# A two-layer encoder whose down projection works with seven products: sums of activations made in other rows, summed weight chunks taken ahead of chained ones

## The chip, the cores and the metric

The kernel runs on one core of one Trainium2 chip. A core has a matrix engine (TensorE, PE in the profile, with its weight loads shown as PEld), a vector engine (VectorE, DVE), an activation engine (ScalarE, ACT), GpSimd (POOL) and a sync engine (SyncE, SP) that here only issues DMAs. Each engine works through its own queue of instructions. Where an instruction needs the result of another engine, it waits at the head of its queue, and what stands behind it waits too. Matrix products are accumulated in PSUM. Operands lie in SBUF, and the weights come from HBM by DMA.

The metric is device microseconds of one execution. Lower is better.

## The reference

Two layers work on x of 256 positions by 2048 features. The even layer mixes by pooling and attention and the odd one by an mLSTM. Neither is touched. Each layer ends in a gated MLP (5632 hidden features), and the change lies there:

```
def conv_ffn(x, w_up, conv_w, conv_b, w_down):
    u = x @ w_up                                  # 2048 -> 2 x 5632
    up = jnp.pad(u, ((0, 0), (1, 1), (0, 0)))
    u = c[0] * up[:, :-2] + c[1] * up[:, 1:-1] + c[2] * up[:, 2:] + conv_b
    gate, val = jnp.split(u, 2, axis=-1)
    return (jax.nn.silu(gate) * val) @ w_down     # 5632 -> 2048

x = x + conv_ffn(rms_norm(x, norm_ffn[layer]), w_up[layer], conv_w[layer], conv_b[layer], w_down[layer])
```

Everything is float32 in the reference.

## The kernel before, in words

**Precision.** A float32 operand is split into a high part (a cast to the matrix engine's format) and a low part (the rest), and a product is made of three matmuls: high by high, high by low, low by high. For a weight chunk of 128 by 1024 the high part is a cast on ScalarE (line 127) and the low part a subtraction on VectorE (line 128). Both write one tile named `hl`, of which there are four. So a chunk can be split only after TensorE is done with the one four before it. The class `Stream` holds the list of chunks in the order in which TensorE takes them. It loads them up to five ahead into six tiles `w` (line 107, SyncE's queue) and splits them up to two ahead.

**The MLP.** The 44 tiles of hidden features are worked through in groups of 4, 8, 8, 8, 8, 8 (`FCH`), called c = 0 to 5. For one tile, `up` makes a group of 64 matmuls from four weight chunks (gate and value). Its result then goes through these steps: `gather` copies one half from PSUM (ACT line 426) and adds the other (DVE line 427), VectorE multiplies by the norm (line 983), ScalarE makes six scaled copies (lines 988 to 990, twice each), VectorE adds them with a shift of one position (lines 991 and 992), then come silu (ACT 996), the product with the value (DVE 997), and the high and low parts (ACT 998, DVE 999).

**The down projection.** For the hidden tiles of c = 0 to 4 a pair of hidden tiles, two halves of 128 positions and two blocks of 512 output columns form a two-by-two block product, which is made with seven block products instead of eight. This needs sums of activations and sums of weights. `combine` (called "mix" in the plan) makes the four sums of activations of one pair: `sf` on VectorE (lines 1005 to 1007), high parts on ScalarE (line 1011) and low parts on VectorE (line 1012), into `s3` (three sums) and `s1` (the fourth).

The products of one group are made in units. A unit A makes the four products 4, 6, 5, 3 of its pairs, and a unit B the three products 0, 1, 2. For the column half h = 1, a unit A takes two kinds of weight chunks for each pair:

- a summed chunk (`Sum`): one block is loaded by SyncE (line 112) and another is added to it on the way by a DMA of GpSimd (line 113), in a tile `sum`, of which there are three. It serves products 4 and 6.
- a chained chunk (`Chain`): it is loaded like any weight. VectorE then adds half of the summed chunk to its first half (line 123, kept on VectorE's queue behind the low part of the chunk before by `behind`) and the first half to the second (line 124), before it is split. It serves products 5 and 3.

For h = 0 both are read ready made from a buffer in HBM (`Made`), which DMAs fill earlier (`premix`, line 472).

**The plan.** `_ffn_plan` writes the order out: a row is one `up`, then at most one unit of the group before (in the first groups sometimes a plain block of the down projection too), then the mixes of that row. Where both column halves go by seven products (c = 2, 3, 4 in layer 0 and c = 1 to 4 in layer 1, `BOTH`), a unit has two pairs. Group c is then multiplied in the eight rows of group c + 1: A for h = 1 with pairs 0, 1 and then 2, 3 (rows 0 and 1), B likewise (rows 2 and 3), then A and B for h = 0 (rows 4 to 7). After the last unit of an A or a B, `drain` adds the accumulated products from PSUM to x or to `acc` (DVE line 1068). Elsewhere a unit has one pair. There are seven groups with units of two pairs and h = 1, so seven rows 0 and seven rows 1 of this kind.

**What sets the order.** TensorE's queue is the order of the program. The other engines' queues are put in order by the framework's scheduler, from its own picture of when an operand is ready, so an instruction's place in the source does not fix its place on VectorE or ScalarE.

Of the kernel before, what the change touches and what calls it, by code (L numbers as in the profile page):

```python
# [9 lines left out]
F32 = mybir.dt.float32  # L10
# [6 lines left out]
P = 128  # L17
# [21 lines left out]
ATT_PARTS = [[4 + h for h in range(8)], [0, 1, 2, 3], [4 + h for h in range(8, 12)]]  # L39
ML_PARTS = [list(range(12)), list(range(12, 16))]  # L40

NG = 4 * KT
# [43 lines left out]
class Stream:  # L86


    def __init__(self, nc, behind, wpool, spool, srcs, load_ahead, split_ahead):
        self.nc, self.behind, self.wpool, self.spool, self.srcs = nc, behind, wpool, spool, srcs  # L90
        self.la, self.sa = load_ahead, split_ahead
        self.w, self.hl = {}, {}
        self.n_load = self.n_split = self.at = 0
# [16 lines left out]
    def prepare(self, i):  # L110
        w = self.sums.tile([P, CH * P], F32, tag="sum", bufs=3, name=f"sum{i}")
        self.nc.sync.dma_start(w, self.srcs[i].one)
        self.nc.gpsimd.dma_start(w, self.srcs[i].other, accum_op=ALU.add)
        self.w[i] = w, CH * P, CH * P

    def split(self, then=None):
        i = self.n_split
        w, n, width = self.w.pop(i)
        if isinstance(self.srcs[i], Sum):
            self.sum = w  # L120
        elif isinstance(self.srcs[i], Chain):
            half = CH * P // 2
            self.behind(self.nc.vector.tensor_add(w[:, :half], w[:, :half], self.sum[:, :half]), self.low)
            self.nc.vector.tensor_add(w[:, half:], w[:, half:], w[:, :half])
        hl = self.spool.tile([P, 2, CH * P], F32R, tag="hl", name=f"hl{i}")
        for c in range(0, width, n):
            (self.nc.vector.tensor_copy if i + c == 0 else self.nc.scalar.copy)(hl[:, 0, c : c + n], w[:, c : c + n])  # L127
            self.low = self.nc.vector.tensor_sub(  # L128
                hl[:, 1, c : c + n], w[:, c : c + n], hl[:, 0, c : c + n].bitcast(F32))
            then and then(c // n)  # L130
        self.hl[i] = hl
        self.n_split += 1
# [76 lines left out]
def trunk(ctx: ExitStack, tc: tile.TileContext, gx, xT, xn, call, catt, cml, weights, mixes, out):  # L209
# [79 lines left out]
    class Norm:  # L289
# [48 lines left out]
        def finish(self):  # L338
            n = self.n
            yield from wv.wait(lambda: self.blocks == NB)  # L340
            s2 = smp.tile([P, 2], F32, tag="nsum", name=f"nsum{n}")
            v.tensor_reduce(s2, self.ss, AX.X, ALU.add)
            self.rcol = rsqrt(s2, 2, 1.0 / D, f"n{n}")
            yield 2.5
            if n % 2 == 0:
                rr = dram.tile([2, P], F32, tag="rr", name=f"rr{n}")
                g.dma_start(rr.rearrange("t p -> p t"), self.rcol)
                R = sm1.tile([P, S], F32, tag="R", name=f"R{n}")
                g.dma_start(R.rearrange("p (t q) -> p t q", t=2), rr.unsqueeze(0).to_broadcast([P, 2, P]))
                self.R = R  # L350
                return
            dg = sm1.tile([P, 2, P], F32, tag="dg", name=f"dg{n}")
            for t in range(2):
                v.tensor_scalar_mul(dg[:, t, :], ident, self.rcol[:, t : t + 1])
            yield 1.0
            pr = psp.tile([P, 512], F32, tag="ps", name=f"npr{n}")
            mm(pr[:, 0:S], ones, dg.rearrange("p a b -> p (a b)"), True, True)
            R = sm1.tile([P, S], F32, tag="R", name=f"R{n}")
            v.tensor_copy(R, pr[:, 0:S])
            self.R = R  # L360
# [121 lines left out]
    def attention_layer(norm, nxt):  # L482
        with ExitStack() as es:
# [73 lines left out]
            def head(h, qt, hh, kt, vt, rq):  # L557
# [3 lines left out]
                for t in range(2):  # L561
# [4 lines left out]
                    mm(sc[:, t, :], q_l, kt[:, 0, kv, :], False, t == 1)  # L566
                mx = smp.tile([P, 2], F32, tag="mx", name=f"mx{h}")
                v.tensor_reduce(mx, sc, AX.X, ALU.max)
                sl = rq[:, :, h % 4]
                v.scalar_tensor_tensor(mx, mx, -1.0, sl, ALU.mult, ALU.mult)  # L570
                pr = tp.tile([P, 2, S], F32, tag="pr", name=f"pr{h}")
                sm = smp.tile([P, 2], F32, tag="sm", name=f"sm{h}")
                for t in range(2):
# [74 lines left out]
            def q_block(ps, qb, gap):  # L648
# [7 lines left out]
                rq = yield from block(ps, 0, dst, f"q{qb}")  # L656
                rs = smp.tile([P, 8], F32, tag="rs", name=f"rs{qb}")
                v.tensor_scalar_mul(rs, rq, HD ** -0.5)
# [96 lines left out]
    def mlstm_layer(norm, nxt):  # L755
        with ExitStack() as es:
# [85 lines left out]
            def head(h, q, kk, vt, hh):  # L842
# [13 lines left out]
                for t in range(2):  # L856
                    for e in range(2):
# [3 lines left out]
                        mm(qk[:, t, :], q_l, kk[:, 0, e, :], False, t == 1 and e == 1)  # L861
                den = smp.tile([P, 4], F32, tag="den", name=f"den{h}")
# [3 lines left out]
                r = smp.tile([P, 4], F32, tag="denr", name=f"denr{h}")  # L866
                v.scalar_tensor_tensor(r, den, -1.0, den, ALU.mult, ALU.max)
# [18 lines left out]
                for t in range(2):  # L886
                    for s_ in range(2):
# [4 lines left out]
                        mm(av[:, t, :], a_l, vh, False, t == 1 and s_ == 1)  # L892
                ss = smp.tile([P, 2], F32, tag="hss", name=f"hss{h}")
                hn = tp.tile([P, 2, MD], F32, tag="hn", name=f"hn{h}")
# [66 lines left out]
    def ffn_layer(layer, norm, nxt):  # L961
        with ExitStack() as es:
# [38 lines left out]
            def combine(c, j):  # L1001
# [20 lines left out]
            def unit(kind, c, h, js):  # L1022
# [12 lines left out]

                todo = []
                for j in js:
# [193 lines left out]
def _ffn_plan(layer):  # L1231
# [6 lines left out]
    for c, n in enumerate(FCH):  # L1238
# [44 lines left out]
def _ffn_weights(layer, up, parts):  # L1283
# [3 lines left out]
    for kind, c, i, *j in _ffn_plan(layer):  # L1287
# [5 lines left out]
        elif kind != "mix":  # L1293
# [118 lines left out]
```

## Time and profile before

| | |
|---|---|
| time, median of three runs | 2193.97 us (2193.04 to 2194.8) |
| the profiled execution | 2193.08 us, of which 2191.3 us from the first to the last instruction |
| TensorE | busy 2168.9 us (99% of the span), 11424 matmuls |
| VectorE | busy 1737.5 us (79%) |
| ScalarE | busy 1405.1 us (64%) |
| mean granted TensorE clock | 0.997 |

Busy times are shares of the whole span. How much room an engine has at one place is read from the timeline of that place. In the timeline a line is an engine's run of equal instructions: start, duration in us, engine, source line, operation, tile written from tiles read, shapes, count, and in brackets the idle time ahead of it with what ended it. Instructions of one engine overlap a little, so the time that one takes from its queue is the distance to the start of the next.

### The profile page before, as it was taken

What the parts mean: (1) busy time and instruction counts of PE and PEld (TensorE: products, weight loads), DVE (VectorE), ACT (ScalarE), POOL (GpSimd) and SP (SyncE); (2) the same over time, 40 slices, a digit from 0 to 9 for tenths busy, and PEclk for the clock granted to TensorE, in tenths of its full rate; (3) what the DMA queues carried; (4) which work ended last, traced back from release to release, by engine and by line L of the source; (5) the groups of instructions that cost most, each with busy time, mean ns of one, the idle gap of its engine ahead of it and who ended that gap; (6) DMA issues with size and microseconds to landing.
All of it is one profiled execution on the core that took longest, in us unless ns stands there. A gap on an engine that the chain in (4) does not pass through costs nothing.

```text
span 2191.3 us, 31590 instructions
## 1 busy us (share of the span) xinstructions
PE 2168.9 (99%) x11424; PEld 1851.9 (85%) x11424; DVE 1737.5 (79%) x2428; ACT 1405.1 (64%) x2200; POOL 128.4 (6%) x160
## 2 busy tenths in 40 slices
PE   9999999999999999999999999999999999999999
PEld 8888888888788888889888888888888888888887
DVE  7686688887888988976777676668888898898896
ACT  7665576767676767666455554457676767676773
POOL 0021010000000000000000000101000000000000
PEclk9999999999999999999999999999999999999999
DMA  9678988797988876767688888999978787887674
GB/s 324 216 209 256 284 252 258 235 272 230 293 274 263 279 244 218 252 195 224 203 254 249 253 241 237 283 272 252 271 202 279 249 271 243 249 268 238 217 252 165
DMA packets 157791, 543.73 MB, mean 248 GB/s; under 512 B 17498, under 2 KB 19842, under 8 KB 157634
## 3 DMA queue, kind: packets, MB, share of 16 engines
q1 hardware_dynamic: 129056, 460.10, 62.0%
q0 software_dynamic: 17440, 48.51, 13.5%
q10 hardware_dynamic: 11138, 33.11, 4.8%
q8 instruction: 89, 1.46, 0.3%
q14 instruction: 68, 0.56, 0.1%
HBM read 539.50 MB, written 60.86 MB: 274 GB/s over the span
## 4 chain that ended last, share of the span: by engine, by line
PE 92%; DVE 4%; issue 2%; ACT 2%; ACTq 0%; DVEq 0%
PE up L263 41%; PE pp L263 12%; PE op L263 8%; PE dn L263 5%; PE mv L263 4%; PE mq L263 4%; PE mk L263 4%; PE mo L263 4%; PE qproj L263 3%; DVE hl L128 2%; PE kproj L263 1%; PE vproj L263 1%; PE pool L263 1%; ACT hl L127 1%; PE qk L263 1%
## 5 line engine op out<-in xcount | busy, mean ns | idle before, releaser
L128 DVE TENSOR_TENSOR hl<-w,hl 128x1024 fp32r<-128x1024 f32 (+2 forms) x836 | 1000.7, 1212 | 234.3 <-ACT hl L127 231.4
L127 ACT CAST hl<-w 128x1024 fp32r<-128x1024 f32 (+2 forms) x835 | 853.6, 1043 | 456.7 <-PE up L263 131.7
L263 PE MATMUL up<-xx,hl 128*128 128x512 f32 (+1 forms) x5632 | 998.5, 338 | 0.3
L263 PEld LDWEIGHTS up<-xx,hl 128*128 128x128 f32 x5632 | 870.6, 189 | 133.0 <-DVE hl L128 1.6
L263 PE MATMUL pp<-hl,s 128*128 128x512 f32 x768 | 197.5, 396 | 16.3 <-ACT hl L127 11.0
L263 PEld LDWEIGHTS pp<-hl,s 128*128 128x128 f32 x768 | 141.0, 188 | 50.1 <-ACT hl L127 14.0
L263 PE MATMUL pp<-hl,g 128*128 128x512 f32 x576 | 149.9, 395 | 0.0
L426 ACT COPY tb_up<-up 128x512 f32<-128x512 f32 x88 | 51.6, 586 | 114.8 <-PE up L263 114.8
L263 PEld LDWEIGHTS pp<-hl,g 128*128 128x128 f32 x576 | 106.4, 189 | 21.0
L263 PE MATMUL dn<-hl,g 128*128 128x512 f32 x528 | 122.7, 390 | 0.0
L991 DVE TENSOR_TENSOR y<-y,z 128x510 f32<-128x510 f32 x88 | 60.7, 690 | 71.2 <-ACT y L990 71.1
L263 PEld LDWEIGHTS dn<-hl,g 128*128 128x128 f32 x528 | 98.7, 188 | 20.4
L990 ACT ACTIVATE y<-tb_up,cst 128x256 f32<-128x256 f32 x176 | 103.8, 590 | 0.0
L427 DVE TENSOR_TENSOR tb_up<-up,tb_up 128x512 f32<-128x512 f32 x88 | 60.6, 689 | 44.4 <-ACT tb_up L426 44.3
L988 ACT ACTIVATE z<-tb_up,cst 128x256 f32<-128x256 f32 x176 | 88.5, 503 | 6.0 <-DVE tb_up L983 4.7
L263 PE MATMUL mk<-xx,hl 128*128 128x512 f32 (+1 forms) x512 | 92.1, 337 | 0.0
L263 PE MATMUL mq<-xx,hl 128*128 128x512 f32 (+1 forms) x512 | 92.1, 337 | 0.0
L263 PE MATMUL mv<-hl,xx 128*128 128x512 f32 (+2 forms) x480 | 91.7, 350 | 0.0
L263 PE MATMUL op<-hl,cat 128*128 128x512 f32 x384 | 91.6, 393 | 0.0
L263 PE MATMUL mo<-hl,xx 128*128 128x512 f32 x384 | 90.5, 391 | 0.0
L263 PE MATMUL op<-hl,mcat 128*128 128x512 f32 x384 | 89.5, 392 | 0.0
L263 PEld LDWEIGHTS mq<-xx,hl 128*128 128x128 f32 x512 | 79.2, 188 | 11.6
(232 smaller groups left out, 2098.4 us busy)
## 6 DMA issues: line engine op xcount, KB each, us to landing
w<-in_up SPq DMA_DIRECT2D x352, 512.0 KB, 4.8
w<-in_dn SPq DMA_DIRECT2D x176, 512.0 KB, 4.5
w<-in_m_in SPq DMA_DIRECT2D x124, 512.0 KB, 5.5
m<-in_dn ACTq DMA_DIRECT2D x56, 512.0 KB, 6.4
w<-m SPq DMA_DIRECT2D x56, 512.0 KB, 4.9
w<-in_a_in SPq DMA_DIRECT2D x46, 512.0 KB, 4.9
sum<-in_dn SPq DMA_DIRECT2D x36, 512.0 KB, 5.5
sum<-in_dn POOLq DMA_DIRECT2D x36, 512.0 KB, 8.7
```

Source lines behind the costliest of these rows:

```text
L127: (self.nc.vector.tensor_copy if i + c == 0 else self.nc.scalar.copy)(hl[:, 0, c : c + n], w[:, c : c + n])
L128: self.low = self.nc.vector.tensor_sub(hl[:, 1, c : c + n], w[:, c : c + n], hl[:, 0, c : c + n].bitcast(F32))
L263: last_mm[0] = pe.matmul(out_, lhsT, rhs, start=start, stop=stop, skip_group_check=True)
L426: a.copy(tb, ps[:, :, 1, :])
L427: v.tensor_add(tb, ps[:, :, 0, :], tb)
L988: a.activation(z[:, 0, j, :], u[:, j, :], AF.Copy, scale=cw(tl, 0))
L990: a.activation(y[:, j, :], u[:, j, :], AF.Identity, scale=cw(tl, 1), bias=cw(tl, 3))
L991: v.tensor_add(y[:, :, 1:S], y[:, :, 1:S], z[:, 0, :, 0 : S - 1])
```

## The change

There are four parts.

1. The sums of activations are made in other rows (`MIX`). Before, the four mixes of a group of eight stood after rows 1, 3, 5, 7 of their group, or after rows 4, 4, 5, 7 where units of the group before hold the buffers. Now they stand after row 4 (pair 0), row 6 (pairs 1 and 2) and row 0 of the next group (pair 3), there behind the unit of that row.
2. A unit A of two pairs takes its chunks in the order summed, summed, chained, chained, where it was summed, chained, summed, chained. TensorE's order of products follows: 4, 6 of both pairs and then 5, 3 of both pairs. The list of chunks, for h = 0 too, is written in that order. Units B and units of one pair keep theirs.
3. Summed chunks wait in a list until their chained chunk comes, and there are four tiles `sum` instead of three.
4. Room for the fourth tile: two of the four `s1` tags have one tile instead of two, `dg` of the norm uses the tile `sq`, and some small tiles (`mx`, `sm`, `rs`, `den`, `denr`, `hss`) come from their stage's own pool.

In the changed kernel the lines up to `combine` and `drain` are numbered 6 higher (128 becomes 134, 1068 becomes 1074).

```diff
+MIX = {(0, 1): [(0, 0)], (0, 3): [(0, 1)]}
+for _c in range(1, len(FCH) - 1):
+    MIX.update({(_c, 4): [(_c, 0)], (_c, 6): [(_c, 1), (_c, 2)], (_c + 1, 0): [(_c, 3)]})
...
-        w = self.sums.tile([P, CH * P], F32, tag="sum", bufs=3, name=f"sum{i}")
+        w = self.sums.tile([P, CH * P], F32, tag="sum", bufs=4, name=f"sum{i}")
...
         if isinstance(self.srcs[i], Sum):
-            self.sum = w
+            self.summed.append(w)
         elif isinstance(self.srcs[i], Chain):
             half = CH * P // 2
-            self.behind(self.nc.vector.tensor_add(w[:, :half], w[:, :half], self.sum[:, :half]), self.low)
+            one = self.summed.pop(0)
+            self.behind(self.nc.vector.tensor_add(w[:, :half], w[:, :half], one[:, :half]), self.low)
             self.nc.vector.tensor_add(w[:, half:], w[:, half:], w[:, :half])
...
-            dg = sm1.tile([P, 2, P], F32, tag="dg", name=f"dg{n}")
+            dg = sm1.tile([P, 512], F32, tag="sq", name=f"dg{n}")[:, : 2 * P].rearrange("p (a b) -> p a b", a=2)
...
-                mx = smp.tile([P, 2], F32, tag="mx", name=f"mx{h}")
+                mx = tp.tile([P, 2], F32, tag="mx", name=f"mx{h}")
...
-                s1 = st.sums.tile([P, 2, P], F32R, tag=f"s1{j}", name=f"s1{layer}_{c}_{j}")
+                s1 = st.sums.tile([P, 2, P], F32R, tag=f"s1{j}", bufs=2 - j % 2, name=f"s1{layer}_{c}_{j}")
...
-                todo = []
+                todo = [[], []]
                 for j in js:
                     s3, s1 = combos[c, j]
                     if kind == "A":
                         xs = [[s3[:, i, m] for i in range(2)] for m in (1, 0, 2)] + [part(j, 1, 1)]
                     else:
-                        xs = [part(j, 0, 0), part(j, 1, 0)]
-                    todo += [(e, x_, j) for e, x_ in zip(order, xs)]
-                if kind == "B":
-                    todo += [(2, [combos[c, j][1][:, i] for i in range(2)], j) for j in js]
+                        xs = [part(j, 0, 0), part(j, 1, 0), [s1[:, i] for i in range(2)]]
+                    for m, (e, x_) in enumerate(zip(order, xs)):
+                        todo[m // 2].append((e, x_, j))
+                todo = sum(todo, [])
...
-        busy = {j: k for k, slot in enumerate(slots) for u in slot if u[0] == "A" for j in u[3]}
         for i in range(n):
             seq.append(("up", c, i))
             seq += slots[i] if i < len(slots) else []
-            if c < len(FCH) - 1:
-                seq += [("mix", c, j) for j in range(n // 2) if i == max(2 * j + 1, busy.get(j, 0))]
+            seq += [("mix", e, j) for e, j in MIX.get((c, i), ())]
...
-            for q in js:
-                if i:
-                    out += [Sum(s0[q], s1[q]), Chain(r[q])]
-                else:
-                    made = [Made(), Made()]
-                    mixes.append((s0[q], s1[q], r[q], made))
-                    out += made
+            if i:
+                out += [Sum(s0[q], s1[q]) for q in js] + [Chain(r[q]) for q in js]
+                continue
+            made = [[Made(), Made()] for _ in js]
+            mixes += [(s0[q], s1[q], r[q], m) for q, m in zip(js, made)]
+            out += [m[e] for e in range(2) for m in made]
```

More of the change, by code (lines that the diff above doesn't have):

```diff
@@ L91, in __init__ @@
         self.la, self.sa = load_ahead, split_ahead
-        self.w, self.hl = {}, {}
+        self.w, self.hl, self.summed = {}, {}, []
         self.n_load = self.n_split = self.at = 0
@@ L571, in head @@
                 pr = tp.tile([P, 2, S], F32, tag="pr", name=f"pr{h}")
-                sm = smp.tile([P, 2], F32, tag="sm", name=f"sm{h}")
+                sm = tp.tile([P, 2], F32, tag="sm", name=f"sm{h}")
                 for t in range(2):
@@ L656, in q_block @@
                 rq = yield from block(ps, 0, dst, f"q{qb}")
-                rs = smp.tile([P, 8], F32, tag="rs", name=f"rs{qb}")
+                rs = tp.tile([P, 8], F32, tag="rs", name=f"rs{qb}")
                 v.tensor_scalar_mul(rs, rq, HD ** -0.5)
@@ L861, in head @@
                         mm(qk[:, t, :], q_l, kk[:, 0, e, :], False, t == 1 and e == 1)
-                den = smp.tile([P, 4], F32, tag="den", name=f"den{h}")
+                den = tp.tile([P, 4], F32, tag="den", name=f"den{h}")
                 for i, (t, d, c, n, o) in enumerate(blocks):
@@ L865, in head @@
                                            ALU.mult, ALU.mult, accum_out=den[:, i : i + 1])
-                r = smp.tile([P, 4], F32, tag="denr", name=f"denr{h}")
+                r = tp.tile([P, 4], F32, tag="denr", name=f"denr{h}")
                 v.scalar_tensor_tensor(r, den, -1.0, den, ALU.mult, ALU.max)
@@ L892, in head @@
                         mm(av[:, t, :], a_l, vh, False, t == 1 and s_ == 1)
-                ss = smp.tile([P, 2], F32, tag="hss", name=f"hss{h}")
+                ss = tp.tile([P, 2], F32, tag="hss", name=f"hss{h}")
                 hn = tp.tile([P, 2, MD], F32, tag="hn", name=f"hn{h}")
```

## The prediction

> **What bounds the kernel now.** I read the groups of instructions on TensorE first, then the waits, then the timeline of one place where TensorE waits, then the granted clock around it.
>
> ```profile
> PE 2168.9 (99%) x11424; PEld 1851.9 (85%) x11424; DVE 1737.5 (79%) x2428; ACT 1405.1 (64%) x2200; POOL 128.4 (6%) x160
> ...
> L263 PE MATMUL pp<-hl,s 128*128 128x512 f32 x768 | 197.5, 396 | 16.3 <-ACT hl L127 11.0 <-DVE hl L128 5.3
> ```
>
> ```profile
> PE pp L263 <- ACT hl L127: 11.0, 7, 1.7
> ```
>
> TensorE is the bound, and the change leaves its matmuls as many as they are. Nearly all its idle time, 16.3 us, lies in seven places of the same kind: the products of a unit A wait once for a chunk's high part (ScalarE) and once for its low part (VectorE). The timeline shows one of the seven, row 0 of c = 4 in layer 0; TensorE first, then VectorE, then ScalarE.
>
> ```profile
> 685.31 2.24 PE L263 MATMUL pp<-hl,s 128*128 128x512 f32 x9
> ...
> 688.08 1.54 PE L263 MATMUL pp<-hl,s 128*128 128x512 f32 x6
> 691.30 0.50 PE L263 MATMUL pp<-hl,s 128*128 128x512 f32 x1 [1.68 <-ACT hl L127]
> 692.56 1.22 PE L263 MATMUL pp<-hl,s 128*128 128x512 f32 x2 [0.76 <-DVE hl L128]
> ```
>
> ```profile
> 675.37 0.69 DVE L991 TENSOR_TENSOR y<-y,z 128x510 f32<-128x510 f32 x1 [0.80 <-ACT y L990]
> ...
> 680.17 1.22 DVE L128 TENSOR_TENSOR hl<-sum,hl 128x1024 fp32r<-128x1024 f32 x1
> ...
> 682.50 0.42 DVE L997 TENSOR_TENSOR s<-s,y 128x256 f32<-128x256 f32 x1
> 682.84 0.68 DVE L1068 TENSOR_TENSOR x<-x,pp 128x512 f32<-128x512 f32 x1
> ...
> 685.03 0.29 DVE L1007 TENSOR_TENSOR sf<-sf,s 128x128 f32<-128x128 f32 x1
> 685.29 1.23 DVE L128 TENSOR_TENSOR hl<-w,hl 128x1024 fp32r<-128x1024 f32 x1
> 686.43 1.22 DVE L128 TENSOR_TENSOR hl<-sum,hl 128x1024 fp32r<-128x1024 f32 x1
> ...
> 688.77 0.75 DVE L1012 TENSOR_TENSOR s<-sf,s 128x384 fp32r<-128x384 f32 x2
> 689.44 0.68 DVE L124 TENSOR_TENSOR w<-w 128x512 f32<-128x512 f32 x1
> 690.04 0.68 DVE L983 TENSOR_TENSOR tb_up<-tb_up,R 128x512 f32<-128x512 f32 x1
> 691.28 3.50 DVE L128 TENSOR_TENSOR hl<-w,hl 128x1024 fp32r<-128x1024 f32 x3 [0.55 <-ACT hl L127]
> ```
>
> ```profile
> 690.20 3.88 ACT L127 CAST hl<-w 128x1024 fp32r<-128x1024 f32 x4 [2.91 <-issue]
> 693.99 0.51 ACT L988 ACTIVATE z<-tb_up,cst 128x256 f32<-128x256 f32 x1
> ...
> 696.59 1.03 ACT L127 CAST hl<-w 128x1024 fp32r<-128x1024 f32 x1
> ```
>
> The unit starts at 685.31. A chunk serves six matmuls (1.39 us, half of 688.08 - 685.31), so the fourth chunk's high part is due at 689.47 and its low part 0.23 us later, at 689.70. They come at 691.30 and 692.56: TensorE loses 2.9 us. VectorE is the cause. From the first split (680.17) to the end of its work ahead of the fourth (line 983, 690.04 and 0.60 more) it does not rest. Distances between starts give its prices: a split 1.14 (686.43 less 685.29; its result is there after 1.22), a 512-wide operation 0.60 (690.04 less 689.44), a 256-wide one 0.34 (682.84 less 682.50), a 128-wide one 0.26 (685.29 less 685.03), the two of line 1012 together 0.67 (689.44 less 688.77). Where an operation needs the one just ahead of it, 0.72 (708.21 less 707.49, in the rows of row 1 below). ScalarE meanwhile waits 2.91 us for the chained weights that VectorE has yet to add up.
>
> Behind some of these places the granted clock halves:
>
> ```profile
> 689.20:692.60 3.40, 0.96 (x4) 0.23 (x2) 2.85 (x6) 2.40 (x3) 0.53 (x1) 0.99 0.95 160
> 692.60:696.00 3.40, 3.40 (x9) 2.72 (x10) 3.31 (x3) 3.40 (x7) 0.86 (x1) 0.51 0.95 239
> 822.30:825.70 3.40, 1.46 (x5) 1.01 (x6) 2.84 (x4) 3.31 (x4) 0.00 (x0) 1.00 0.77 136
> 825.70:829.10 3.40, 3.40 (x12) 2.82 (x11) 2.59 (x4) 3.40 (x8) 0.00 (x0) 0.50 0.95 271
> ...
> 1767.80:1771.20 3.40, 3.40 (x12) 2.81 (x11) 2.60 (x4) 3.40 (x8) 0.85 (x1) 0.51 0.91 280
> ...
> 2030.60:2034.00 3.40, 3.40 (x11) 2.75 (x10) 2.93 (x3) 3.40 (x8) 0.00 (x0) 0.50 0.71 219
> 559.40:562.90 3.50, 1.94 (x7) 1.41 (x8) 2.99 (x4) 3.50 (x5) 0.00 (x0) 1.00 1.01 214
> ```
>
> The columns are PE, PEld, DVE, ACT, POOL busy, the clock, and DMA. A 3.4 us stretch in which TensorE was busy 0.96 or 1.46 us is followed by 3.4 us at half clock one with 1.94 us is not. There are four stretches at half clock, each worth 3.4 x 0.5 = 1.7 us.
>
> **The change, part by part.** The built order of the changed kernel decides here, since neither the plan's rows nor the order of chunks bind VectorE and ScalarE by themselves. At the place above (h1 to h4 are the splits of the four chunks) their queues stand so, with the old line numbers:
>
> ```
> VectorE  h1, 1068, 997, 1068, h2, 123, 1005, 999, 124, 1006, 427, 1007, 983,
>          h3, 123, 1012 x2, 124, 991, 992, h4
> ScalarE  h1, 996, h2, 998, 426, h3, 1011 x2, 988, 989, 990, 988, 989, 990, h4
> ```
>
> *The mix of pair 3* (1005 to 1007, 1012) stands in row 0 behind the unit by the plan, but ahead of h4 by the queue, as before: its inputs are ready, so it is taken. That edit gains nothing here.
>
> *The order of chunks* trades places: h2 needs no chain now, h3 does. Both chains are still made in front of h4. What stands ahead of h4 is the same work as before, 10.47 us (680.17 to 690.64), plus the two shifted adds 991 and 992 of the new `up`. Those stood behind h4 before.
>
> Step by step, with the first split at 680.17 as before (what stands ahead of it is the same, and VectorE's 0.80 us wait for ScalarE ahead of it absorbs the mixes moved from row 5): two splits, two 1068, 997, 123, 1005, 999, 124, 1006 take 2.28 + 1.20 + 0.34 + 0.60 + 0.34 + 0.34 + 0.60 + 0.26 = 5.96, to 686.13. Line 427 needs ScalarE's copy of what TensorE has just finished. Row 1 prices that (TensorE, ScalarE, then VectorE):
>
> ```profile
> 706.53 2.24 PE L263 MATMUL pp<-hl,s 128*128 128x512 f32 x9
> 706.73 0.59 ACT L426 COPY tb_up<-up 128x512 f32<-128x512 f32 x1 [1.74 <-PE up L263]
> 707.65 2.00 ACT L127 CAST hl<-w 128x1024 fp32r<-128x1024 f32 x2 [0.33 <-DVE w L124]
> 707.49 0.68 DVE L427 TENSOR_TENSOR tb_up<-up,tb_up 128x512 f32<-128x512 f32 x1
> 708.21 0.69 DVE L983 TENSOR_TENSOR tb_up<-tb_up,R 128x512 f32<-128x512 f32 x1
> 708.81 2.35 DVE L128 TENSOR_TENSOR hl<-w,hl 128x1024 fp32r<-128x1024 f32 x2
> ```
>
> So 427 can start 0.96 us into the unit (707.49 - 706.53), here 686.27. With 427, 1007, 983 (1.46) h3 starts at 687.73 and ends at 688.95. TensorE wants the third chunk's low part at 688.08 + 0.23 = 688.31 and waits 0.7 us, a new wait. Then, from 688.87, 123, 1012, 124 (1.87) run to 690.74, with the result at 690.82. ScalarE's six copies start when 983 is done (687.9) and take 2.6 us (696.59 less 693.99), to 690.5: they are out of the way in time, and the cast of h4 runs from 690.9 to 691.95. But 991 (0.72, since 992 needs it) and 992 (0.60) put h4's low part from 692.06 to 693.28. TensorE's second matmul of chunk four starts 0.06 behind it as before (692.56 less 692.50), at 693.34 instead of 692.56: **0.78 us later**, the stall 3.6 us instead of 2.9. Five places have this queue.
>
> In layer 0's first such place (row 0 of c = 3; 427 stands two places further ahead there, 992 behind h1) the wait for 427 falls earlier in the queue:
>
> ```profile
> 554.15 2.24 PE L263 MATMUL pp<-hl,s 128*128 128x512 f32 x9
> ...
> 561.46 0.72 PE L263 MATMUL pp<-hl,s 128*128 128x512 f32 x2 [0.76 <-DVE hl L128]
> 548.91 1.22 DVE L128 TENSOR_TENSOR hl<-sum,hl 128x1024 fp32r<-128x1024 f32 x1
> ```
>
> 427 cannot start before 555.1 (554.15 + 0.96) though the queue is there at 554.2 (1.14 + 0.60 + 0.60 + 1.14 + 0.60 + 0.34 + 0.60 + 0.34 behind 548.91). The rest of the way to h4 is 6.2 us (427, 999, 1006, 983, h3, 123, 1007, 1012, 124, 991, 992), so h4 runs from 561.3 to 562.6 and TensorE goes on at 562.6, 1.2 us later. In the seventh place (layer 1, row 0 of c = 2) 991 and 992 already stand ahead of h1 in both kernels and the sum ahead of h4 is the same: 0. Row 0 together: 5 x 0.78 + 1.2 = **+5.1 us**. Ends: 0 (the same work ahead of h4, the adds hidden) and 6 x 1.32 = 7.9 (both adds in full).
>
> *Row 1*, pairs 2 and 3, seven times. Now the queue is 123, 427, 124, 983, h4: the last chain's second add stands behind the wait for 427. Counted from the unit's start by the rows of row 1: 427 at 0.96, 124 from 1.56 to 2.24, the cast from 2.3 to 3.35, h4 from 3.4 to 4.6, while the low part is due at 4.16 + 0.23 = 4.39. Before it was there at 3.5 (708.81 + 1.22 - 706.53). A wait of about 0.24: 7 x 0.24 = **+1.7 us**, between 0 and 7 x 0.6 = 4.2 (124 a whole place later).
>
> *The half clock.* Of six full stalls four were followed by it. The longer idle of 0.7 + 1.8 + 1.1 us leaves less than 1.5 us busy in a 3.4 us stretch for most positions; I take five: **+1.7 us**, between -6.7 (none) and +5.1 (all seven). [...]
>
> *The rest.*
>
> ```profile
> 668.56 1.22 DVE L128 TENSOR_TENSOR hl<-w,hl 128x1024 fp32r<-128x1024 f32 x1 [1.22 <-ACT hl L127]
> 670.88 0.69 DVE L427 TENSOR_TENSOR tb_up<-up,tb_up 128x512 f32<-128x512 f32 x1 [1.10 <-ACT tb_up L426]
> ```
>
> ```profile
> w<-in_dn SPq DMA_DIRECT2D x176, 512.0 KB, 4.5
> ```
>
> Two mixes in row 6 are 3.1 us of VectorE (each 0.34 + 0.26 + 0.26 + 0.67), and the unit B there has three chunks to split instead of four. In the built order they spread over rows 6 and 7, where VectorE has the two waits above and the 0.80 us further on: nothing for TensorE. If that cover were gone, row 0's first split would be late by up to 3.1 - 2.3 = 0.8 us, and the stall with it (5 us over six places). In rows 4 to 6 for h = 0 no place of TensorE's waiting lies before, and the order of ready-made chunks changes nothing. Four `sum` tiles let SyncE issue the next summed loads sooner. The last chained chunk of row 1 takes the tile that h4 leaves at 693.3, is there some 4.5 us later and is wanted 11 us on: nothing. `dg` and the small tiles lie off TensorE's path.
>
> Sum: 2193.1 (the profiled execution: 2191.3 span and 1.8 around it) + 5.1 + 1.7 + 1.7 = 2201.6 us. The median of the runs is 0.9 us above the profiled one, so 2202.
>
> **The rivals.** *A: the order works (faster).* If h4 came 2.9 us sooner than before, as when 991, 992 and pair 3's mix gave way to it, seven stalls (16.3 us and the part inside matmuls, 2.9 each, about 19) and the half clock (6.7) go: 2193 - 26 = 2167. For it: ScalarE's 2.91 us of idle there. Against: the queue above. Deciding point: h4's low part done by 4.39 us into the unit. *B: no change.* The adds are hidden in the 0.55 us wait before h4, and row 1 keeps its slack: 2193 to 2196. *C: three short waits in place of two long ones leave more than 1.9 us busy in every stretch, and the clock never halves:* 2201.6 - 8.4 = 2193.2. For: the idle is cut in more pieces. Against: two of them, 1.8 and 1.1, still lie 0.23 us apart. [...] *D: row 1 stalls in earnest* (0.6 each) *and all seven rows 0 lose the clock:* 2201.6 + 2.5 + 3.4 = 2207.5.
>
> **How the numbers follow.** A measurement of this kernel can tell about 0.2%, 4.4 us, from no change. The forecast (2198.4 to 2206) 0.66, D 0.08, B 0.11, C 0.06, A 0.09. Slower 0.74, same 0.17, faster 0.09. The range 2192 to 2208 holds all but A.
>
> **What would show it.** Right: idle of TensorE before `pp<-hl,s` above 16.3 us, three waits in six rows 0 with a new one of about 0.7 us at the third chunk, small waits in row 1, 991 and 992 in front of h4. Wrong: two waits or none there, h4 ahead of 991, fewer than four stretches at half clock.

## The result, and the profile after

The changed kernel takes 2206.45 us (median of four runs, 2205.45 to 2209.31) against 2193.97 before. The ratio is 1.0059, with an interval of 1.0042 to 1.0077: slower, as forecast, and 4.5 us above the predicted 2202, just above the forecast's own 2198.4 to 2206. The profiled execution took 2205.82 us (span 2204.0), 12.7 us above that of before.

The busy times and TensorE's group of products, and then TensorE's waits, of the changed kernel (in a row of the waits: total us, count, longest):

```profile
PE 2177.2 (99%) x11424; PEld 1852.6 (84%) x11424; DVE 1734.8 (79%) x2428; ACT 1408.3 (64%) x2200; POOL 129.6 (6%) x160
...
L269 PE MATMUL pp<-hl,s 128*128 128x512 f32 x768 | 203.4, 401 | 21.0 <-DVE hl L134 10.9 <-ACT hl L133 10.1
```

```profile
PE pp L269 <- DVE hl L134: 10.9, 20, 0.8
PE pp L269 <- ACT hl L133: 10.1, 7, 1.6
```

TensorE has the same 11424 matmuls. The seven waits for a high part are still there. The waits for a low part went from 7 to 20: six new ones at the third chunk of row 0 and seven in row 1.

Row 0 of c = 4 in layer 0 again, by the timeline; TensorE, VectorE, ScalarE:

```profile
689.48 3.20 PE L269 MATMUL pp<-hl,s 128*128 128x512 f32 x13
692.97 0.74 PE L269 MATMUL pp<-hl,s 128*128 128x512 f32 x2 [0.30 <-DVE hl L134]
...
695.97 0.49 PE L269 MATMUL pp<-hl,s 128*128 128x512 f32 x1 [1.56 <-ACT hl L133]
697.31 0.89 PE L269 MATMUL pp<-hl,s 128*128 128x512 f32 x2 [0.84 <-DVE hl L134]
```

```profile
691.10 0.68 DVE L989 TENSOR_TENSOR tb_up<-tb_up,R 128x512 f32<-128x512 f32 x1
691.70 1.22 DVE L134 TENSOR_TENSOR hl<-w,hl 128x1024 fp32r<-128x1024 f32 x1
...
694.11 0.68 DVE L130 TENSOR_TENSOR w<-w 128x512 f32<-128x512 f32 x1
...
695.43 0.69 DVE L998 TENSOR_TENSOR y<-y,z 128x510 f32<-128x510 f32 x1
696.03 3.49 DVE L134 TENSOR_TENSOR hl<-w,hl 128x1024 fp32r<-128x1024 f32 x3
```

```profile
694.87 2.94 ACT L133 CAST hl<-w 128x1024 fp32r<-128x1024 f32 x3 [0.36 <-ACT y L996]
```

There are three waits now. TensorE goes on with the fourth chunk's second matmul 7.83 us after the unit's start (697.31 - 689.48), where before it was 7.25 (692.56 - 685.31). The fourth split starts at 696.03; its cast, 1.05 us long, has ended only at 695.92.

Row 1 of the same group:

```profile
711.29 3.67 PE L269 MATMUL pp<-hl,s 128*128 128x512 f32 x15
...
716.30 0.73 PE L269 MATMUL pp<-hl,s 128*128 128x512 f32 x2 [0.42 <-DVE hl L134]
```

```profile
704.25 1.23 DVE L134 TENSOR_TENSOR hl<-sum,hl 128x1024 fp32r<-128x1024 f32 x1 [1.78 <-ACT hl L133]
707.03 1.23 DVE L134 TENSOR_TENSOR hl<-sum,hl 128x1024 fp32r<-128x1024 f32 x1 [1.56 <-ACT hl L133]
708.18 0.68 DVE L129 TENSOR_TENSOR w<-w,sum 128x512 f32<-128x512 f32 x1
...
710.83 1.23 DVE L134 TENSOR_TENSOR hl<-w,hl 128x1024 fp32r<-128x1024 f32 x1 [1.25 <-ACT hl L133]
711.98 0.68 DVE L129 TENSOR_TENSOR w<-w,sum 128x512 f32<-128x512 f32 x1
...
715.02 3.50 DVE L134 TENSOR_TENSOR hl<-w,hl 128x1024 fp32r<-128x1024 f32 x3 [0.56 <-ACT hl L133]
```

```profile
703.17 1.05 ACT L133 CAST hl<-sum 128x1024 fp32r<-128x1024 f32 x1 [1.74 <-PE up L269]
705.96 1.05 ACT L133 CAST hl<-sum 128x1024 fp32r<-128x1024 f32 x1 [1.74 <-PE up L269]
```

VectorE idles 1.78 and 1.56 us, each time for a cast that itself waited for TensorE (1.74 us) to be done with a tile, and then has both chains still to make, one after the other: add (708.18), add, cast, third split (710.83), add (711.98), add, cast, fourth split (715.02). The first adds of both chains could have run in those idle times (with a looser tie, below, they do), but `behind` keeps each behind the split of the chunk ahead of it, and those splits wait for TensorE to free a tile. In the old order a summed chunk, which needs no adds, stands between the two chains; in the new one two tied chains follow each other, 4.2 us from split to split (715.02 - 710.83), while TensorE takes a chunk in 1.39 us. The low part comes 5.0 us into the unit and is due at 4.39.

The clock, in stretches of 3.4 us (columns as in the prediction: length, PE, PEld, DVE, ACT, POOL busy, clock, DMA):

```profile
557.80:561.20 3.40, 1.54 (x6) 0.97 (x6) 3.40 (x8) 3.33 (x8) 0.87 (x1) 1.00 0.56 200
561.20:564.60 3.40, 2.68 (x6) 1.79 (x7) 3.40 (x4) 3.01 (x4) 0.00 (x0) 0.50 1.02 192
564.60:568.00 3.40, 3.40 (x12) 2.81 (x11) 3.13 (x5) 1.45 (x2) 0.85 (x1) 0.50 1.02 339
694.30:697.70 3.40, 0.99 (x4) 0.54 (x4) 3.37 (x5) 3.04 (x4) 0.00 (x0) 1.00 0.93 230
697.70:701.10 3.40, 3.40 (x11) 2.73 (x10) 3.40 (x5) 2.50 (x5) 0.00 (x0) 0.50 1.03 325
...
2039.20:2042.60 3.40, 1.76 (x6) 0.88 (x6) 3.37 (x7) 3.04 (x6) 0.00 (x0) 1.00 0.42 154
2042.60:2046.00 3.40, 2.63 (x13) 2.24 (x14) 3.40 (x4) 3.40 (x5) 0.00 (x0) 1.00 0.46 148
```

Five places are followed by half clock, one of them (561.2) for two stretches: six stretches, where before had four.

The 12.7 us, from distances between starts of TensorE's matmuls (what is above the usual distance): the five rows 0 of one kind 0.47 + 1.73 + 1.11 = 3.30 us each against 2.88, the row of c = 3 in layer 0 3.72 against 2.93, the seventh 1.97 against 2.02, together 2.8; row 1 seven times 0.59 to 0.67, 4.25; two stretches of half clock, 3.4. That is 10.5. The rest, 2.2 us, lies outside these places, and part of it is pace, in steps too small to be seen as waits. From 844.22 to 1629.38 us of before, a stretch without a unit A of two pairs for h = 1, the profile of after took 785.81 us where before took 785.17. The old order with the tie two and three back (below) took 785.17 too, the two other old-order kernels below 785.54 and 785.59 (0.4 of it at one place), and every kernel below in the new order 785.8 or more, so it goes with the program and not with the run. The same rate over the whole length would be 1.8 us, as an estimate. The stretch does hold parts of the change (chunks of h = 0 in the new order, small tiles in their new places). Which of them sets the pace is not known.

### The profile page after: what moved, and what is told of

It reads as the page before. It is cut to its first block, busy times and chain, and to the rows that moved or that the text cites. A ratio compares the mean times of both kernels' runs of the same rounds, so it can differ in the third digit from the quotient of the medians.

```text
span 2204.0 us, 31578 instructions
## 1 busy us (share of the span) xinstructions
PE 2177.2 (99%) x11424; PEld 1852.6 (84%) x11424; DVE 1734.8 (79%) x2428; ACT 1408.3 (64%) x2200; POOL 129.6 (6%) x160
## 4 chain that ended last, share of the span: by engine, by line
PE 93%; DVE 5%; ACT 2%; issue 0%; ACTq 0%; DVEq 0%
PE up L269 42%; PE pp L269 12%; PE op L269 8%; PE dn L269 5%; PE mv L269 4%; PE mq L269 4%; PE mk L269 4%; PE mo L269 4%; PE qproj L269 3%; DVE hl L134 2%; ACT hl L133 1%; PE kproj L269 1%; PE vproj L269 1%; PE pool L269 1%; DVE w L130 1%; DVE w L129 1%
## 5 line engine op out<-in xcount | busy, mean ns | idle before, releaser
L269 PE MATMUL pp<-hl,s 128*128 128x512 f32 x768 | 203.4, 401 | 21.0 <-DVE hl L134 10.9
```

The lines of the kernel that those rows point to most:

```text
L269: last_mm[0] = pe.matmul(out_, lhsT, rhs, start=start, stop=stop, skip_group_check=True)
```

## The experiments

The theory from this comparison: the order of chunks alone makes the loss, by way of the tie (`behind`) that holds a chain's first add behind the split ahead of it. The rivals were the mixes' rows and the shifted adds (the prediction's own reading). Line numbers of the variants are up to two higher than in the changed kernel.

**The mixes' rows alone.** The kernel before, with the new rows.

```diff
...
-            if c < len(FCH) - 1:
-                seq += [("mix", c, j) for j in range(n // 2) if i == max(2 * j + 1, busy.get(j, 0))]
+            seq += [("mix", e, j) for e, j in MIX.get((c, i), ())]
```

> The kernel before with only the rows of the mixes moved. Theory O (the order of chunks costs the time, the rows of the mixes nothing): 2194 us, within 2, because VectorE's queue ahead of the fourth split is that of the kernel before, and the waits in the seven rows 0 stay 1.7 and 0.8 us, none in row 1. Rival M (the moved mixes load VectorE ahead of row 0): 2198 us or more, with a longer wait in rows 0.

2193.32 us, ratio 1.0001 (0.9991 to 1.001). TensorE's group:

```profile
L267 PE MATMUL pp<-hl,s 128*128 128x512 f32 x768 | 197.6, 396 | 16.3 <-ACT hl L131 11.0 <-DVE hl L132 5.3
```

The same waits as before. The rows cost and bring nothing.

**The order of chunks alone.** The changed kernel with the old rows, `s1` as before and three `sum` tiles.

```diff
-            seq += [("mix", e, j) for e, j in MIX.get((c, i), ())]
+            if c < len(FCH) - 1:
+                seq += [("mix", c, j) for j in range(n // 2) if i == max(2 * j + 1, busy.get(j, 0))]
...
-        w = self.sums.tile([P, CH * P], F32, tag="sum", bufs=4, name=f"sum{i}")
+        w = self.sums.tile([P, CH * P], F32, tag="sum", bufs=3, name=f"sum{i}")
...
```

> The changed kernel with the mixes in their old rows, the s1 tiles as before and three sum tiles. Theory O: 2206 us, within 3, with waits of about 0.5, 1.7 and 1.1 us in six rows 0 and 0.6 us in rows 1, as in the changed kernel. Rival M: 2195 to 2200. If the fourth sum tile matters (a third one is free only when a chained chunk has used it), summed chunks come late and the time is above 2209.

2207.74 us, ratio 1.0065 (1.005 to 1.008), with the waits of the changed kernel:

```profile
L265 PE MATMUL pp<-hl,s 128*128 128x512 f32 x768 | 203.5, 402 | 21.3 <-DVE hl L130 11.2 <-ACT hl L129 10.1
```

The new order of chunks makes the whole loss without the new rows, and the fourth tile changes nothing. The small tiles (part 4 of the change, `s1` aside) stay in this kernel, so no run parts them from the order. But from the first matmul of the key projection to the first product of a unit, attention included, TensorE takes 309.03 us in the profiles of before and of after alike (5.30 to 314.33 and 5.05 to 314.08), and for the mLSTM, up to its output projection, 461.32 and 461.48 us: the stages that use them changed by 0.2 us at most.

**The chain's first add left free.** The changed kernel without the tie.

```diff
-            self.behind(self.nc.vector.tensor_add(w[:, :half], w[:, :half], one[:, :half]), self.low)
+            self.nc.vector.tensor_add(w[:, :half], w[:, :half], one[:, :half])
```

> The changed kernel without the note that keeps a chain's first add behind the split before it. Theory O, second part (in row 1 both chains wait behind the second summed split, which itself waits for TensorE's tile): the adds move into VectorE's waits, the 0.6 us in rows 1 go (4.2 us), and in row 0 what stands ahead of the fourth split shrinks from 11.7 us to about 6, so the waits of 3.3 us and the half clock go as well: about 2172 us. Rival W (VectorE has too much work over the whole row, wherever it stands): the wait turns up at another chunk and the time stays between 2195 and 2206.

2181.57 us, ratio 0.9948 (0.9933 to 0.9962): faster than both kernels, and no stretch at half clock. But not the gain in full: a free add is put so early that it meets a load that has not landed, at the head of VectorE's queue. TensorE's waits, and one such place on VectorE:

```profile
PE up L269 <- DVE hl L134: 5.5, 7, 2.2
```

```profile
1632.17 0.69 DVE L129 TENSOR_TENSOR w<-w,sum 128x512 f32<-128x512 f32 x1 [3.54 <-DMA w<-in_dn]
```

1.7 us of waits are left ahead of the products; the others have moved to `up`, whose chunks' splits stand behind that add. So the tie has a use, and is too tight for the new order.

**The shifted adds last.** The changed kernel, with 991 and 992 (997 and 998 there) of a row 0 behind the unit's last split.

```diff
+                add = v.tensor_add(y[:, :, 1:S], y[:, :, 1:S], z[:, 0, :, 0 : S - 1])
+                late and behind(add, st.lows[st.at - 1])
...
```

> The changed kernel with the two shifted adds of row 0 put behind the low part of the fourth split. The prediction's step (the adds delay the low part by 0.72 + 0.60): the low part comes 1.3 us sooner at most and 0.7 us at least, so 2201 to 2202 us. Theory O as the trace of the changed kernel has it (the fourth split waits for its cast, which follows the chain's second add, and the adds only fill that wait): 0.1 us a place, 2205 to 2207 us.

2210.94 us, ratio 1.008 (1.0065 to 1.0095). VectorE in the same place:

```profile
694.51 0.69 DVE L131 TENSOR_TENSOR w<-w 128x512 f32<-128x512 f32 x1
696.35 1.23 DVE L135 TENSOR_TENSOR hl<-w,hl 128x1024 fp32r<-128x1024 f32 x1 [1.16 <-ACT hl L134]
```

With the adds gone VectorE stands still for 1.16 us ahead of the split and waits for the cast. TensorE's last wait falls by 0.08 us (1.11 to 1.03). The adds were hidden. The time rose by the clock: nine stretches at half clock where the changed kernel has six, 5.1 us of the 5.5 between the two profiled executions. Neither expectation had that.

**The norm multiply last.** The changed kernel, with line 989 of a row 0 behind the last chain's second add.

```diff
+                mul = v.tensor_mul(u, u, bc(norm.R, 2))
+                late and behind(mul, st.chained[st.at - 1])
...
```

> The changed kernel, with the norm multiply (line 989 there) put behind the last chain's second add in the seven rows 0. Theory N (that multiply is what delays the chain in row 0, since it moved ahead of the second add; the shifted adds are hidden): the second add comes 0.6 us sooner after the unit's start, the cast and the fourth split with it, and the waits of a row 0 sum to 2.7 us instead of 3.3. Row 1 keeps its 0.6 us each. Six rows by 0.6 are 3.6 us: 2202 to 2203 us, or down to 2198 if two or three stretches at half clock go with it. Rival K (what ends last is the third split and the cast behind it, not the multiply): waits of 3.3 us as before, 2206 us. Rival L (the multiply is missed by ScalarE, whose six copies then run after the cast): row 1's waits grow above 0.6 us, 2206 or more.

2203.87 us, ratio 1.0049 (1.0032 to 1.0065). TensorE in that row 0:

```profile
688.87 3.78 PE L270 MATMUL pp<-hl,s 128*128 128x512 f32 x15
...
694.91 0.49 PE L270 MATMUL pp<-hl,s 128*128 128x512 f32 x1 [1.56 <-ACT hl L134]
696.17 1.22 PE L270 MATMUL pp<-hl,s 128*128 128x512 f32 x2 [0.77 <-DVE hl L135]
```

The wait at the third chunk is gone, the fourth chunk's second matmul starts 7.30 us into the unit (before 7.25), and the waits sum to 2.77 us. So it is the multiply, standing ahead of the third split and the second chain, that made row 0 worse. The time fell less than expected (2202 to 2203): the six stretches at half clock stay, and the waits of a row 1 are no longer 0.6 us each but 0.45 to 0.90, once 0.45 + 1.03, 1.1 us more in sum.

**The tie taken from the kernel before.** One line in the old order of chunks.

```diff
-            self.behind(self.nc.vector.tensor_add(w[:, :half], w[:, :half], self.sum[:, :half]), self.low)
+            self.nc.vector.tensor_add(w[:, :half], w[:, :half], self.sum[:, :half])
```

> The kernel before (order summed, chained, summed, chained) with one thing changed: the chain's first add is no longer kept behind the low part of the chunk ahead of it. Theory H (the tie of the add to the split ahead of it is what costs, in either order): TensorE's waits before the products of a unit A fall from 16.3 us to under 4, no stretch at half clock is left (6.7 us), and some of it comes back as waits of `up` chunks, as it did in the changed order (5.5 us): 2193.2 - 12 - 7 + 5 = 2179, between 2174 and 2184 us. Rival G (the new order of chunks is needed for it, since only there both sums are loaded and split before a chain asks for them): in the old order the early add waits for the second summed chunk's load at the head of VectorE's queue, everything behind it is late, and the time is 2190 or more.

2177.23 us, ratio 0.9925 (0.991 to 0.994), faster than the changed kernel with the same freedom. VectorE's group of those adds, and TensorE's waits:

```profile
L123 DVE TENSOR_TENSOR w<-w,sum 128x512 f32<-128x512 f32 x36 | 24.8, 688 | 31.6 <-DMA w<-in_dn 28.4 <-DMA sum<-in_dn 3.2
```

```profile
PE up L263 <- DVE hl L128: 5.9, 10, 1.5
...
PE up L263 <- ACT hl L127: 1.1, 1, 1.1
```

VectorE waits 31.6 us for loads, and TensorE's waits ahead of `up` come to 7.0 us. The tie held the old order back as well.

**The tie two and three chunks back.** The changed kernel, with the add behind an earlier split.

```diff
-            self.behind(self.nc.vector.tensor_add(w[:, :half], w[:, :half], one[:, :half]), self.low)
+            self.behind(self.nc.vector.tensor_add(w[:, :half], w[:, :half], one[:, :half]), self.lows[i - 2])
...
```

> The changed kernel with the chain's first add kept behind the low part of the chunk two ahead of it in the list instead of that just ahead of it. Theory T (the tie costs because it lies behind a split that waits for TensorE to free a tile; one chunk further back it is loose enough, and not so loose that the add meets an unfinished load): row 1's 4.2 us of waits go, the waits of a row 0 fall from 3.3 to about 2.0 us, no VectorE wait for a load of more than 1 us appears: 2206 - 4.2 - 6 x 1.3 = 2194 us with as many stretches at half clock as now, 2184 with none. Rival W (any earlier add meets its load at the head of VectorE's queue, as with the add left free): waits before `up` of 5 us, 2181 to 2187 with waits of row 0 under 1 us.

2179.31 us, ratio 0.9937 (0.9922 to 0.9952). Row 1 on VectorE and on TensorE:

```profile
700.27 0.68 DVE L130 TENSOR_TENSOR w<-w,sum 128x512 f32<-128x512 f32 x1
700.87 0.68 DVE L131 TENSOR_TENSOR w<-w 128x512 f32<-128x512 f32 x1
...
701.81 0.68 DVE L131 TENSOR_TENSOR w<-w 128x512 f32<-128x512 f32 x1
702.80 1.22 DVE L135 TENSOR_TENSOR hl<-w,hl 128x1024 fp32r<-128x1024 f32 x1 [0.31 <-ACT hl L134]
```

```profile
703.03 3.67 PE L270 MATMUL pp<-hl,s 128*128 128x512 f32 x15
...
707.23 0.86 PE L270 MATMUL pp<-hl,s 128*128 128x512 f32 x3
```

Both chains are done in the time in which VectorE used to idle, before the unit starts, and TensorE has no wait in row 1. Most rows 0 wait 0.74 + 0.45 us, less than the 2.0 expected, and the time is below both expectations; there is no half clock, and VectorE waits for no load of a chunk of `w_down`.

> As with two back, but the chain's first add is kept behind the low part three ahead of it; nothing else of the changed kernel is touched. Theory T (what stands on VectorE's queue ahead of the fourth split sets the wait; one 0.6 us add more is taken out of that stretch): the waits of a row 0 fall from 0.74 + 0.45 us to about 0.6 in sum, 2179.3 - 6 x 0.6 = 2175.7 us, between 2174 and 2178. Rival W (it is loose enough now to meet unfinished loads): waits of VectorE for loads above 5 us in sum, waits before `up`, 2180 or more.

Three back: 2175.83 us, ratio 0.9919 (0.9904 to 0.9934), row 0 at 0.74 + 0.24 us. The step was 3.5 us where 3.6 was expected, but not for the reason given: the waits fell by 0.2 us per row 0, where 0.6 was expected, and the idle time ahead of these products by 2.0 us in all (5.2 to 3.2).

**Norm multiply and pair 3's mix late, with the tie as it is.**

```diff
+                mul = v.tensor_mul(u, u, bc(norm.R, 2))
+                late and behind(mul, st.lows[st.at - 1])
...
+                first = v.tensor_sub(sf[:, 0:2], g4[:, 0::3], g4[:, 1:2].to_broadcast([P, 2, P]))
+                after is not None and behind(first, after)
...
```

> The changed kernel with its tie of the chain's first add as it is; only the norm multiply of rows 0 and 1 and the mix of pair 3 are put behind the low part of the unit's fourth chunk. Theory Q (the wait is the sum of what stands ahead of the fourth split): in row 0 the norm multiply and pair 3's mix (0.60 + 0.34 + 0.26 + 0.26 + 0.67 us) leave that stretch, part of it only covered a wait for the third split's tile; the waits of a row 0 fall from 3.3 to about 2 us and the new one at the third chunk goes; row 1 stays at 0.6 us: 2206 - 6 x 1.3 - 2 to 10 for the half clock = 2188 to 2196 us. Rival T (only the tie matters): 2202 or more.

2200.88 us, ratio 1.0033 (1.0021 to 1.0045), between the two expectations. Most rows 0 wait 1.18 + 1.03 us, about as expected, but row 1 grew at four of its seven places (0.17 to 0.44, then 1.03 us), and four stretches at half clock stayed. Shortening the queue alone does not pay for the tie.

**Both.** The tie three back and the rest late.

> The changed kernel with the chain's first add behind the low part three ahead of it, and with the norm multiply of rows 0 and 1 and the mix of pair 3 behind the low part of the unit's fourth chunk. Theory Q (what stands on VectorE's queue ahead of the fourth split sets the stall; taken out, the order of chunks does what it could): the waits before the products of a unit A fall to under 3 us, no half clock, no wait for a load of over 1 us: 2193.2 - 16 - 6.7 and some = 2168 to 2175 us, faster than with the add left free (2181.6). Rival V (what is put late is missed: ScalarE's six copies, the mix's sums for the unit B): new waits before `up` or before the unit B, 2180 us or more.

2172.84 us (2172.47 to 2173.17), ratio 0.9907 (0.9892 to 0.9921): faster than both kernels, by 20 us than the kernel before. TensorE's group and its row 0:

```profile
L270 PE MATMUL pp<-hl,s 128*128 128x512 f32 x768 | 196.8, 396 | 0.2
```

```profile
682.76 3.96 PE L270 MATMUL pp<-hl,s 128*128 128x512 f32 x15
686.55 0.86 PE L270 MATMUL pp<-hl,g 128*128 128x512 f32 x3
687.25 0.85 PE L270 MATMUL pp<-hl,s 128*128 128x512 f32 x3
```

Idle time ahead of these products is 0.2 us in the whole kernel. One wait of VectorE for a load is left, 1.1 us.

**The old order with looser ties.** The kernel before with the tie two back, and then the best version in the old order (with the new rows for the mixes).

> The kernel before (old order of chunks, old rows) with the chain's first add behind the low part two ahead of it. Theory H (the tie is what costs, whatever the order): in the old order one first add of 0.6 us leaves the stretch ahead of the fourth split, the waits of a row 0 fall from 2.4 to about 1.8 us and most stretches at half clock go: 2193.2 - 6 x 0.6 - 3 to 7 = 2183 to 2187 us. Rival G (the new order is what makes the looser tie worth something): 2190 or more, against 2179.3 in the new order with the same tie.

2188.08 us, ratio 0.9978 (0.9968 to 0.9987), between the two expectations. By distances between starts most rows 0 wait 1.53 + 1.03 us where before had 1.86 + 1.03, about half of the fall that was expected, and three rows 1 have a new wait of 0.39. Most of the gain is the clock: one stretch at half speed where before had four, 5.1 of the 7.0 us between the profiled executions.

> The best version so far (tie three back, norm multiply and pair 3's mix late) in the old order of chunks, with the mixes in their new rows: what differs from it is the order of chunks alone (and three summed tiles for four). Theory O (the order of chunks buys nothing by itself once the queue ahead of the fourth split is short): within 2 us of 2172.8. Rival P (the new order leaves the chain more time, since its sum is there two chunks ahead): waits before the products of a unit A or loads met at the head of VectorE's queue, 2176 us or more.

2174.25 us, ratio 0.9912 (0.9898 to 0.9927), by its interval not to be told apart from the best version. Its second chunk, chained in the old order, is late by a little in row 0:

```profile
684.29 0.51 PE L268 MATMUL pp<-hl,s 128*128 128x512 f32 x1 [0.23 <-ACT hl L132]
685.55 0.72 PE L268 MATMUL pp<-hl,s 128*128 128x512 f32 x2 [0.76 <-DVE hl L133]
```

Idle ahead of these products is 5.0 us here against 0.2, but the profiled span is only 1.6 us longer (2172.0 against 2170.4). The pace gives the rest back: outside these places the best version loses some 3.5 us in small steps from one group of matmuls to the next, in the stretch from 844.22 to 1629.38 us of before for instance (785.84 us against 785.17). What sets the pace is open, as above.

All of them by order of chunks and by what the first add stands behind (us; the old order has its old rows, except at 2174.25):

| | the chunk ahead | two back | three back | three back, rest late | free |
|---|---|---|---|---|---|
| old order | 2193.97 | 2188.08 | not run | 2174.25 | 2177.23 |
| new order | 2206.45 | 2179.31 | 2175.83 | 2172.84 | 2181.57 |

The new order is 12.5 us worse with the tight tie, 8.8 better with the tie two back, and 4.3 worse with none.

## Why the prediction was right or wrong

**The mechanism** (the built order decides, and no chained split comes sooner) was right. The mixes' rows and the fourth `sum` tile, costed at nothing, cost nothing: the first two experiments. For the small tiles no run shows it by itself; the stages that use them changed by 0.2 us at most.

**Row 0, +5.1, measured +2.8.** The new wait at the third chunk came (0.47 us for 0.7), and TensorE went on at 7.83 us into the unit, forecast 8.03. The failing step is "But 991 (0.72, since 992 needs it) and 992 (0.60) put h4's low part from 692.06 to 693.28." By the prediction's own numbers the cast would end at 691.95, 0.1 us before that, so the adds could hold up nothing; moving them away left the wait within 0.08 us. What made the fourth chunk late is the second add of the last chain, 4.63 us into the unit (694.11 - 689.48) where it was 4.13, because the norm multiply now stands ahead of it. The prediction's sum has that shift in it (its second add starts 4.83 us into the unit, 690.74 - 0.60 - 685.31) but names the adds as the cause, so its 0.78 us came near the measured 0.58 with the wrong reason beside it. In the first such place (c = 3) the prices that it lists sum to 6.4 us, not 6.2; its +1.2 was measured as +0.8. The upper end, "both adds in full", bounded a cost that is not there.

**Row 1, +1.7, measured +4.25, above its bound of 4.2.** The step counted only the wait for 427 ahead of the chain's second add and took the third split as done in time, as before. It is not: it is a chained chunk now, tied behind a split that waits for a free tile, and the fourth chunk's chain is tied behind it in turn. With the tie two back row 1 has no wait at all, so the price of the tie was the missing term.

**Half clock, five stretches, +1.7.** The profiled run has six, +3.4. The direction was right; the count depends on where a wait lies on the grid of 3.413 us on which the half clock came (below), which was not to be had from the sum of idle time.

**The sum.** 2.8 + 4.25 + 3.4 and 2.2 of pace and small waits make 12.7, where 5.1 + 1.7 + 1.7 = 8.5 was forecast. The pace had no term. Row 0's excess hid half of the two shortfalls, which was luck.

**The rivals.** B was right that the adds are hidden, and wrong that nothing else is late. D's row 1 (0.6 each) is what came, without all seven losing the clock, and its 2207.5 is nearest to the result. C fell: three waits in place of two kept the clock halving. A named its deciding point, the fourth low part done 4.39 us into the unit; the best version meets it and runs at 2172.84 (A gave 2167), so the order can work, but only once the tie lets the adds go ahead. The prediction has no term for the tie.

## What to carry to other kernels

What a scheduling hint costs depends on the order of work: taking this one out gained 16.7 us in the old order and 24.9 in the new. When the order changes, ask of each "keep this behind that" what "that" now waits for, here a split held by a full buffer while the engine idled 1.78 and 1.56 us beside it. In the new order the add did best with some of the tie left: three back took 2175.83, tied to the step just ahead 2206.45, and to nothing 2181.57, with a 3.54 us wait at the head of the queue. In the old order none (2177.23) was better than two back (2188.08), so how far back has to be tried. Tying the add to the landing of its own load was not tried. And before work on a queue is charged to what follows, see whether what follows also waits for another engine until the same moment.

## What the runs showed of the hardware

In these runs the half clock came on a fixed grid. Within each run the starts of these stretches lie whole multiples of 3.413 us apart (in the changed kernel 561.19, 697.72 and 830.84: 40 and 39 steps). I laid that grid over the profiles of all fourteen kernels (where there is no stretch, by the drop at the end of the run; in before that drop comes at 2191.0, 439 steps behind the stretch at 692.55) and added up, for each cell, the matmuls that lie in it, at 0.225 us for a 512-wide one and 0.113 for a 256-wide one (one that lies across two cells counts in parts). In before, 18 of 512 in a row took 4.10 us (802.25 to 806.35), 0.228 each, and 32 of each width 11.14 us (1118.30 to 1129.44), 0.174 each. The first 10 us of a run, which the clock's record covers only in part (from 6.47 us on in before, from 4.81 in the changed kernel), and the last cells are left out. All 34 cells with 1.21 us or less of matmuls were followed by half clock, none with 1.41 or more was, and between the two 7 were and 3 were not. So, as an estimate from these cells, it is the matmuls in a cell that count, some 6 of 512 out of the 15 that fit (3.413 / 0.228), and not the idle time of one wait: the 2.8 us of a row 0 with the multiply last and the 2.6 us with the tie two back in the old order gave six stretches and one. A wait that lies across two cells can be free of it. With the tie two back in the old order, two rows 0 with the same waits (1.53 + 1.03 us) differ so, 1.91 us busy in the first cell of the one and 1.27 in that of the other:

```profile
687.30:690.70 3.40, 1.91 (x7) 1.03 (x6) 3.05 (x6) 1.73 (x2) 0.72 (x1) 1.00 0.86 208
690.70:694.10 3.40, 2.77 (x14) 2.36 (x15) 3.40 (x4) 3.40 (x7) 0.86 (x1) 1.00 1.01 239
1888.80:1892.20 3.40, 1.27 (x5) 0.53 (x4) 3.05 (x6) 2.60 (x3) 0.00 (x0) 1.00 0.67 136
1892.20:1895.60 3.40, 3.40 (x10) 2.70 (x10) 3.12 (x3) 3.40 (x8) 0.00 (x0) 0.50 1.03 334
```

In row 0 of c = 4 of the changed kernel, waits of 1.56 and 0.84 us, parted by one matmul, were followed by half clock (from 697.7 on).

The same count fits the stretches that follow each other: in the changed kernel the one at 561.2 was itself stalled and held 1.21 us of matmuls, and the next 3.4 us ran at half clock too, while every half-clock stretch with 1.58 us or more (seven matmuls) was followed by full speed.
